# Small parts of the rwkv projections' weights: split beforehand into DRAM instead of split on arrival

## The chip, the cores and the metric

The kernel runs on one core of a Trainium2 chip. The metric is the time of one execution on the device in microseconds (us); for a kernel it is the median of its runs. PE is the matrix engine, PEld its weight loads, DVE, ACT and POOL are the vector, scalar and GpSimd engines, and SP is the queue from which nearly all DMAs are issued.

## The reference, cut to what matters

Two blocks of two layers each run one after the other on 256 tokens of 1024 features. The first block's second layer is an rwkv mixer; between its first layer's mixer and it lies a squared-relu MLP on tokens and context (512 columns in all):

```
x = x + gt_m * squared_relu_mlp(modulate(x, sh_m, sc_m), mlp_w1[layer], mlp_w2[layer])
ctx = ctx + cgt_m * squared_relu_mlp(modulate(ctx, ...), ...)
...
o_l, o_c = rwkv_mixer(h_l, h_c, rw_mu[j], rw_w_rkv[j], rw_w0[j], rw_w1[j], ...)
```

The mixer forms six mixtures of each token with its neighbours and multiplies them by weights: k, r and v (1024 x 1024 each), and the narrow w1, a1, g1 and g2.

## The kernel before, in words

Every product with weights is done in three passes of float32r: a weight tile is split into a large part `wh` (a cast) and a small part `wl` (the tile less that cast), the activations likewise into `mh` and `ml`, and `mm3` sums wh·mh, wh·ml and wl·mh (L162, L163, L164 are the three matmuls). A tile of weights is 128 x 1024 once split (`HLC` columns) and 128 x 2048 as most are loaded (`WCOL` columns, 1 MB).

In the first MLP the order is that of the code and of the tile framework. ACT casts (L71), DVE subtracts (L72), SP loads (L48). A feature tile of the hidden layer takes 8 weight units; its relu is on ACT (L1871), and ACT also casts the result to `dh` (L167). The results lie in two PSUM banks, `g`. The next layer's modulation (`ada`) is a thread: its matmuls (L1343, 16 tiles) are put between the MLP's first products, a group of four tiles at a time, and its last groups run behind the MLP.

In the rwkv projections (`rwkv_in`) a planner, `Weave`, takes up threads of requests in the order in which it reckons that engines come free, and writes the instructions in that order; each engine and queue then works strictly in it. Threads there are the norm and mixing (`ri_front` L2038 to L2049, `ri_mix` L2063 to L2069), the weights (`wv_weights`), the products (`ri_products`), and behind them the "items" (L2297 to L2425), the elementwise work on decays and keys that prepares the scan. `wv_weights` loads into two raw tiles of 2048 columns, casts on ACT (L445), and subtracts on DVE (L453), or, for each second tile of k and r, on POOL (L450). Split tiles lie in four slots called `whl`, each given back once the last product with it is placed. Some elementwise steps may go to either DVE or POOL; the planner chooses by its own clock.

k's product begins with a lead of four feature tiles, features of the mixture outer and tiles inner: it takes a unit of each of the weight tiles k0 to k3 for every mixed feature. `lww` and `lwa` are the parts of two more small weights (in_rw_w, in_rw_a), needed only behind the products w and a; they pass through the same raw tiles (loaded at L2255, cast at L2257, subtracted at L2260).

Of the kernel before, what the change touches and what calls it, by code (L numbers as in the profile page):

```python
# [13 lines left out]
ALU = mybir.AluOpType  # L14
# [15 lines left out]
class Stream:  # L30
    """A weight matrix as a row of [128, nb] units, loaded in tiles of WCOL
    columns and split into two float32r parts whose sum is exact."""
# [47 lines left out]
class KB:  # L80
    HLC = 1024

    def __init__(self, tc, ins, out, dbg=None):
# [3 lines left out]
        self.pend = []  # L87

# [24 lines left out]
    def open_psum(self, **banks):  # L113
        """all of PSUM: banks per pool"""
# [4 lines left out]
    def open_gemm(self, n=4):  # L119
        """the pools of the products with weights"""  # L120
# [21 lines left out]
    def row_in(self, name, n, pool=None):  # L142
        """a row of n numbers, the same in all partitions"""
# [8 lines left out]
    def act_set(self, after, name):  # L152
        """load a named activation table right behind an instruction"""
# [5 lines left out]
    def mm3(self, ps, wh, wl, xh, xl, start, stop):  # L159
        """ps += (wh + wl).T @ (xh + xl) in three float32r passes"""  # L160
# [9 lines left out]
    def begin(self, g):  # L170
        """runs a generator's first part; the others follow behind later products"""
# [12 lines left out]
    def gemm_a(self, st, nt, kt, xh, xl, evac, n_cols=T, lead=0, cuts=2):  # L184
        """features of the result on partitions; st units [128k, 128n], n outer;
        the first lead tiles take the products in cuts parts, a part of all of them at a time"""
# [9 lines left out]
        for n in range(lead, nt):  # L196
            ps = self.psg.tile([P, 512], F32, name="g")
            o = ps[:, :n_cols]
            for k in range(kt):
                wh, wl = st.next()  # L200
                self.mm3(o, wh, wl, xh(k), xl(k), k == 0, k == kt - 1)
            evac(n, o)

    def gemm_b(self, st, nt, kt, pairs, xh, xl, evac, between=None):
        """tokens of the result on partitions; st units [128k, 256], n outer; one
        bank holds two token tiles"""
# [14 lines left out]
    def rstd_tok(self, sums, n, width, scale, eps):  # L221
        """(sums * scale + eps) ** -0.5 on a [128, n] tile"""
# [7 lines left out]
    def sumsq(self, pool, xs, kt):  # L230
        """for each x the sum over its feature tiles of x squared: [128, T], the partitions still to add"""
# [12 lines left out]
    def rstd_from(self, acc, n_feat):  # L244
        """token-major 1/rms [128, 2] from the squares' partial sums"""
# [5 lines left out]
    def bcast_tok(self, rs, pool, col=0, n=2):  # L251
        """rs [128 tokens, n] -> [128, n * 128], the same row in all partitions"""
# [11 lines left out]
class Phase:  # L264
    """pools of one phase: tag -> number of buffers, opened together"""
# [20 lines left out]
def bc(ap, axis, n):  # L286
    """ap with a new axis of n equal entries at free position axis"""
# [6 lines left out]
class Weave:  # L294
    """Emits threads of work, each a generator of requests, in the order in which the
    engines would take them up. A request comes before the instructions it stands for:
    (engine, us and the latency behind it), ("any", us by engine), ("take", slot) and ("give", (slot, index)), ("set", event) and
    ("wait", event), ("later", us), ("spawn", generator) or ("spawn", generator, us by which it
    lets others go before)."""
# [10 lines left out]
    def settle(self, th):  # L310
        """one request of a thread that needs no engine; whether it could be met"""
# [69 lines left out]
    def load(self, end):  # L381
        """the array's work in the window before a time"""
# [4 lines left out]
    def keep(self, end, work, after=None):  # L387
        """products of no use ahead of work up to a time, where the array's clock would drop"""
# [5 lines left out]
    def add_warm(self, at, n, after=None):  # L394
        """n products of 64 columns"""
# [14 lines left out]
class Second(KB):  # L410
    WOVEN = None

# [1 line left out]
    def wv_open(self, cut=1):  # L414
        """the weights' tiles, held; those loaded into cut in parts"""
        raw = [self.raw.tile([P, WCOL], F32, name="raw") for _ in range(2)]
# [5 lines left out]
    def wv_weights(self, streams, ring="", shared=()):  # L422
        """weights in their order, loaded and split"""
# [36 lines left out]

    def wv_unit(self, name, nb, u):
        """waits for a unit of weights; its parts"""
# [7 lines left out]
    def wv_done(self, name, nb, us, last, ring=""):  # L470
        """gives back the tiles of weights whose last unit is among us"""
# [6 lines left out]
    def pre_norm(self, ph, gain, x=None, tagx="xn"):  # L478
        """splits x * gain; returns the parts and the squares' partial sums"""
# [76 lines left out]
            # gating  # L556
# [36 lines left out]
            # layer norm of g over its 512 features  # L593
# [28 lines left out]
    def gelu(self, ph, out, x, n):  # L622
        """0.5 x (1 + tanh(sqrt(2/pi) (x + 0.044715 x^3))); overwrites x's scratch"""
# [78 lines left out]
    def mem_load(self):  # L702
        """the memory and the squares' sums, for both layers"""
# [2437 lines left out]
```

## Time and profile before

| | us |
|---|---|
| median of 3 runs | 2858.17 |
| lowest and highest run | 2854.01, 2858.56 |
| span of the profiled execution | 2854.8 |
| first MLP | 421 to 783 |
| rwkv projections | 783 to 1054 |

The span goes from the first to the last instruction of one profiled execution. Around the span there is no separate figure: the median of the runs is 3.4 us above it, and a sum made on the span is carried to the median by adding these 3.4 us. A busy engine is no proof of a bound: the stages have different limits, so the sections below go stage by stage.

### The profile page before, as it was taken

What the parts mean: (1) busy time and instruction counts of PE and PEld (TensorE: products, weight loads), DVE (VectorE), ACT (ScalarE), POOL (GpSimd) and SP (SyncE); (2) the same over time, 40 slices, a digit from 0 to 9 for tenths busy, and PEclk for the clock granted to TensorE, in tenths of its full rate; (3) what the DMA queues carried; (4) which work ended last, traced back from release to release, by engine and by line L of the source; (5) the groups of instructions that cost most, each with busy time, mean ns of one, the idle gap of its engine ahead of it and who ended that gap; (6) DMA issues with size and microseconds to landing.
All of it is one profiled execution on the core that took longest, in us unless ns stands there. A gap on an engine that the chain in (4) does not pass through costs nothing.

```text
span 2854.8 us, 52905 instructions
## 1 busy us (share of the span) xinstructions
PE 2654.0 (93%) x22052; PEld 2362.1 (83%) x22052; DVE 1763.1 (62%) x2885; ACT 1297.4 (45%) x2358; POOL 402.5 (14%) x392
## 2 busy tenths in 40 slices
PE   5999999999968879887899999999999999799999
PEld 3977567888757666765899999998999999798999
DVE  4453564334386966885774665776665665765764
ACT  3344333223245541675553544555444444655443
POOL 1210100000044552342100001011001001311100
PEclk9999989999978889998999999999999999999999
DMA  7244735223223675323455455433455554233554
GB/s 274 89 156 152 260 126 191 103 89 104 83 72 107 226 228 114 81 68 96 139 186 179 170 183 198 163 134 119 167 188 177 178 186 172 96 105 110 177 178 148
DMA packets 108142, 426.29 MB, mean 149 GB/s; under 512 B 14334, under 2 KB 50430, under 8 KB 66046
## 3 DMA queue, kind: packets, MB, share of 16 engines
q1 hardware_dynamic: 107326, 420.76, 43.1%
q8 instruction: 173, 2.83, 0.4%
q10 hardware_dynamic: 576, 2.15, 0.2%
q14 instruction: 67, 0.55, 0.1%
HBM read 397.68 MB, written 24.13 MB: 148 GB/s over the span
## 4 chain that ended last, share of the span: by engine, by line
PE 78%; DVE 13%; ACT 4%; POOL 2%; issue 2%; DMA 1%; SPq 0%; ACTq 0%; DVEq 0%; POOLq 0%
PE g L162 20%; PE g L163 20%; PE g L164 20%; PE pG L162 2%; PE pG L163 2%; PE pG L164 2%; DVE pr L2605 2%; DVE N L2607 2%; PE d L1343 2%; PE pX L2623 1%; DVE wl L72 1%; PE pA L2551 1%; POOL acc L495 1%; DVE we L2558 1%; POOL rs L227 1%
## 5 line engine op out<-in xcount | busy, mean ns | idle before, releaser
L72 DVE TENSOR_TENSOR wl<-raw,wh 128x1024 fp32r<-128x1024 f32 x512 | 626.9, 1225 | 427.7 <-ACT wh L71 425.5
L71 ACT CAST wh<-raw 128x1024 fp32r<-128x1024 f32 x512 | 535.2, 1047 | 638.0 <-PE g L163 546.2
L163 PE MATMUL g<-xnl,wh 128*128 128x256 f32 x1504 | 427.9, 285 | 1.0 <-DVE xnl L168 1.0
L162 PE MATMUL g<-xnh,wh 128*128 128x256 f32 x1504 | 427.4, 285 | 1.3 <-ACT xnh L167 1.3
L164 PE MATMUL g<-xnh,wl 128*128 128x256 f32 x1504 | 427.9, 285 | 0.0
L162 PE MATMUL g<-hh,wh 128*128 128x256 f32 (+1 forms) x1216 | 374.4, 308 | 4.9 <-ACT wh L71 3.4
L164 PE MATMUL g<-hh,wl 128*128 128x256 f32 (+1 forms) x1216 | 373.3, 307 | 0.7 <-DVE wl L72 0.7
L163 PE MATMUL g<-hl,wh 128*128 128x256 f32 (+1 forms) x1216 | 373.9, 308 | 0.0
L162 PEld LDWEIGHTS g<-xnh,wh 128*128 128x128 f32 x1504 | 290.5, 193 | 1.7 <-ACT xnh L167 1.7
L163 PEld LDWEIGHTS g<-xnl,wh 128*128 128x128 f32 x1504 | 290.6, 193 | 1.5 <-DVE xnl L168 1.5
L164 PEld LDWEIGHTS g<-xnh,wl 128*128 128x128 f32 x1504 | 290.7, 193 | 0.0
L162 PEld LDWEIGHTS g<-hh,wh 128*128 128x128 f32 x1216 | 234.6, 193 | 17.5 <-ACT wh L71 4.0
L163 PEld LDWEIGHTS g<-hl,wh 128*128 128x128 f32 x1216 | 234.3, 193 | 14.2 <-DVE hl L1382 2.5
L164 PEld LDWEIGHTS g<-hh,wl 128*128 128x128 f32 x1216 | 234.1, 193 | 12.5 <-issue 1.7
L495 POOL TENSOR_TENSOR acc<-acc,sq 128x256 f32<-128x256 f32 x63 | 65.8, 1045 | 863.5 <-ACT sq L494 381.2
L162 PE MATMUL g<-dh,wh 128*128 128x512 f32 (+1 forms) x512 | 172.0, 336 | 0.0
L163 PE MATMUL g<-dl,wh 128*128 128x512 f32 (+1 forms) x512 | 172.0, 336 | 0.0
L164 PE MATMUL g<-dh,wl 128*128 128x512 f32 (+1 forms) x512 | 172.0, 336 | 0.0
L2623 PE MATMUL pX<-ident 128*128 128x256 f32 (+3 forms) x388 | 106.9, 386 | 32.8 <-DVE N L2607 17.9
L163 PE MATMUL g<-wl,hh 128*128 128x256 f32 x448 | 128.4, 287 | 6.9 <-DVE wl L72 6.9
L162 PE MATMUL g<-wh,hh 128*128 128x256 f32 x448 | 131.2, 293 | 3.3 <-ACT wh L71 3.2
L164 PE MATMUL g<-wh,hl 128*128 128x256 f32 x448 | 127.8, 285 | 0.0
(590 smaller groups left out, 5961.7 us busy)
## 6 DMA issues: line engine op xcount, KB each, us to landing
raw<-in_w_mlp SPq DMA_DIRECT2D x64, 1024.0 KB, 4.8
raw<-in_w_ada SPq DMA_DIRECT2D x48, 1024.0 KB, 6.3
raw<-in_w_pre_gu SPq DMA_DIRECT2D x44, 1024.0 KB, 4.8
raw<-in_w_post_gu SPq DMA_DIRECT2D x44, 1024.0 KB, 4.8
raw<-in_w_pre_down SPq DMA_DIRECT2D x22, 1024.0 KB, 4.8
raw<-in_w_post_down SPq DMA_DIRECT2D x22, 1024.0 KB, 4.8
raw<-in_w_ab SPq DMA_DIRECT2D x14, 1024.0 KB, 4.9
d_bk<-h SPq DMA_DIRECT2D x16, 512.0 KB, 3.0
```

The costliest lines, as they stand in the source:

```text
L71: nc.scalar.copy(h[:, :w], r)
L72: nc.vector.tensor_tensor(l[:, :w], r, h[:, :w].bitcast(F32), op=ALU.subtract)
L162: mm(ps, wh, xh, start=start, stop=False)
L163: mm(ps, wh, xl, start=False, stop=False)
L164: mm(ps, wl, xh, start=False, stop=stop)
L227: nc.gpsimd.tensor_tensor(rs[:, :n], ms[:, :n], self.mhalf[:, :n], op=ALU.pow)
L495: nc.gpsimd.tensor_tensor(acc, acc, sq, op=ALU.add)
L1343: nc.tensor.matmul(ps[32 * j : 32 * j + 32], self.cpad[:, k0 + j, 30 - 2 * n : 62 - 2 * n], raw[:, j * 512 : (j + 1) * 512], start=n == 0 ...
L2551: nc.tensor.matmul(ps[64:, i], bk[:64, i0 + i], we[0][:64, :W, i0 + i], start=True, stop=True)
L2605: nc.vector.tensor_tensor(pr, bc(N[:, k + 1 :, k], 2, k), bc(N[:, k, :k], 1, m), op=ALU.mult)
L2607: row = nc.vector.tensor_tensor(N[:, k + 1 :, :k], N[:, k + 1 :, :k], pr, op=ALU.add)
L2623: mm = self.nc.tensor.matmul(o, self.ident, bc(self.ident[:, :64], 1, cols // 64), start=True, stop=True)
```

## The change

Thirty tiles of 128 x 1024, all of k, w1, a1, g1, g2, r and v, get their small parts during the first MLP. A new generator `lows` loads a tile (a DMA of ACT's queue), casts it on ACT, subtracts on DVE and stores the small part to DRAM (again ACT's queue). It moves by one step per eight products of the MLP. In the projections, `wv_ready` loads the raw tile from SP as before, casts it on ACT, and reads the small part from DRAM by a DMA of POOL's queue. No subtraction of these weights is left there. Raw tiles there become two of 1024 columns (one tile cut in two), and the space of the second one becomes a fifth `whl` slot. So that the space for `lows` is free, the rest of the modulation thread is drained at the beginning of the MLP. The planner's order changes with all this.

```diff
 class KB:
+        self.side = None
 def gemm_a(...):
                 self.mm3(o, wh, wl, xh(k), xl(k), k == 0, k == kt - 1)
+                if self.side and k % 8 == 7:
+                    next(self.side, None)
...
+    def wv_ready(self, streams):
...
+                raw = yield "take", "raw"
+                nc.sync.dma_start(w, self.i[src][t, :, c : c + n])
+                q = yield "take", "whl"
+                h, l = self.wt["whl"][q]
+                yield "Pool", 0.5, 0.0
+                nc.gpsimd.dma_start(l[:, :n], self.low[src][t, :, c : c + n])
...
+                    yield "ACT", 0.12 + 0.83 * n / 1024
+                    nc.scalar.copy(h[:, :n], w)
+                    yield "give", ("raw", raw)
...
 def mlp(...):
             self.modulate(ph, self.xs[:ns], mods, 3, self.split_shift(hh, hl), between, (4, 2, 4))
+            if behind:
+                behind()
...
+class Lows(First):
+    LOWS = [("w_rw_k", 64 * P), ("w_rw_w1", 8 * P), ("w_rw_a1", 8 * P), ("w_rw_g1", 16 * P), ("w_rw_g2", 8 * 256), ("w_rw_r", 64 * P),
+            ("w_rw_v", 32 * 256)]
+    def lows(self, ph):
...
+        tile = lambda: ph.tile("lw", [P, self.HLC], F32R)
+        def weights(src, at):
...
+            a = tile()
+            w = a.bitcast(F32)
+            nc.scalar.dma_start(w, self.i[src][t, :, c])
+            yield
+            h = ph.tile("lh", [P, self.HLC], F32R)
+            nc.scalar.copy(h, w)
+            nc.vector.tensor_tensor(a, w, h.bitcast(F32), op=ALU.subtract)
+            yield
+            nc.scalar.dma_start(self.low[src][t, :, c].bitcast(F32), a.bitcast(F32))
+        parts = [weights(n, at) for n, w in self.LOWS for at in range(0, w, self.HLC)]
+        for j in range(len(parts) + 3):
+            for g in parts[max(j - 3, 0) : j + 1]:
+                next(g, None)
+            yield
...
 def rwkv_in(...):
-            self.wv_open(2)
-            w = self.weave = Weave(raw=2, whl=4, ...)
+            self.wv_open(2, 1)
+            more = self.raw.tile([P, WCOL], F32R, name="raw")
+            self.wt["whl"].append([more[:, : self.HLC], more[:, self.HLC :]])
+            w = self.weave = Weave(raw=2, whl=5, G=4, L=2, f=2, xg=3, o=3, kk=3, it=4)
...
-            w.add(self.wv_weights(self.STREAMS, shared="kr"), 0.5)
+            w.add(self.wv_ready(self.STREAMS), 0.5)
...
 def run(self):
+                def behind():
+                    for _ in self.ada:
+                        pass
+                    pa.__exit__(None, None, None)
+                    self.side = self.lows(es.enter_context(self.phase("lo", side=RIGHT, lw=4, lh=2)))
+                self.mlp(0, a0[1], 2, self.ada, behind)
+                for _ in self.side:
+                    pass
```

Line numbers move with it: the MLP's relu L1871 is L1909 in the changed kernel, its cast L167 is L168, the mixing's L2067 is L2141, the items' L2362 is L2436, the power L2220 is L2294. New are L477 (raw load), L482 (DMA of the small part), L488 (cast), and in the MLP L1943 (load), L1946 (cast), L1949 (store).

**ACT's order in the first MLP.** Before, the steady round (r is a relu's result, dh its cast, wh a cast of the MLP's weights):

```order
L1871 ACTIVATE r<-g 128x512 [waits PE_49]
L167 CAST dh<-r 128x512 [waits DVE_49]
L71 CAST wh<-raw 128x1024 [waits DMAHW2_49]
L71 CAST wh<-raw 128x1024 [waits PE_49,Activation_49]
L1871 ACTIVATE r<-g 128x512 [waits PE_49,Activation_49]
L167 CAST dh<-r 128x512 [waits DVE_49]
```

Of the change, in the same place, from the first of the loads of `lows` on (adrow is the last copy of the modulation; lw and lh are the tiles of `lows`):

```order
L1943 DMA lw<-in_w_rw_k 128x1024 [waits DMAHW5_49,DMAHW4_49,DMAHW6_49,DMAHW2_49,DMAHW0_49]
L1943 DMA lw<-in_w_rw_k 128x1024 [waits DMAHW5_49,DMAHW3_49,DMAHW7_49,DMAHW1_49,PE_49]
L1943 DMA lw<-in_w_rw_k 128x1024
L1946 CAST lh<-lw 128x1024 [waits DMAHW6_49,Activation_49]
L1946 CAST lh<-lw 128x1024 [waits DMAHW7_49]
L1943 DMA lw<-in_w_rw_k 128x1024
L1949 DMA low_w_rw_k<-lw 128x1024 [waits DVE_49] x2
L1946 CAST lh<-lw 128x1024 [waits DMAHW0_49,Activation_49]
L1909 ACTIVATE r<-g 128x512 [waits PE_49]
L1946 CAST lh<-lw 128x1024 [waits DMAHW1_49,Activation_49]
```

The relu in the middle now stands behind three casts of `lows`, each of which waits for a load, and behind two stores, each of which waits for DVE. Later in the MLP the order has come to a steady round:

```order
L1943 DMA lw<-in_w_rw_w 128x1024 [waits DMAHW0_49]
L71 CAST wh<-raw 128x1024
L1949 DMA low_w_rw_k<-lw 128x1024 [waits DVE_49]
L1909 ACTIVATE r<-g 128x512 [waits PE_49]
L1946 CAST lh<-lw 128x1024 [waits DMAHW6_49,Activation_49]
L168 CAST dh<-r 128x512 [waits DVE_49]
```

Each round has one load, one store and one cast of `lows` in ACT's queue between the MLP's own three instructions, and the cast waits for the load that opens the round.

**SP's order at the start of the projections.** Before (raw tiles of k hold two tiles of 1024 each):

```order
L434 DMA raw<-in_w_rw_k 128x2048 [waits DVE_49,DMAHW1_49,Activation_49,Pool_49]
L1999 DMA sel<-in_c_sel 128x256 [waits PE_49]
L434 DMA raw<-in_w_rw_k 128x2048 [waits DVE_49,DMAHW2_49,Activation_49,Pool_49]
L2255 DMA raw<-in_rw_w 128x1024 [waits DMAHW7_49,DVE_49]
L2255 DMA raw<-in_rw_a 128x1024 [waits DMAHW3_49,DMAHW1_49,DVE_49]
```

Of the change, from k2's raw load on:

```order
L477 DMA raw<-in_w_rw_k 128x1024 [waits DMAHW7_49,Activation_49]
L2073 DMA sel<-in_c_sel 128x256 [waits DVE_49,PE_49]
L2329 DMA raw<-in_rw_w 128x1024 [waits DMAHW0_49,Activation_49]
L2329 DMA raw<-in_rw_a 128x1024 [waits DMAHW6_49,DMAHW3_49,Activation_49]
L477 DMA raw<-in_w_rw_k 128x1024 [waits DMAHW5_49,DVE_49]
L477 DMA raw<-in_w_rw_k 128x1024 [waits DMAHW6_49,DVE_49]
L477 DMA raw<-in_w_rw_k 128x1024 [waits DMAHW7_49,DMAHW1_49,Activation_49]
```

The loads of in_rw_w and in_rw_a stood behind all of k; now they take the two raw slots behind k2, and the loads of k3 and k4 wait for DVE to have done with them.

**ACT's order there.** Of the change, from the cast of k2 on (mh is a mixed feature's cast; there are 16 of the first mixture in all, and the last two stand here; `raw` as a target is the fifth slot):

```order
L488 CAST wh<-raw 128x1024 [waits DMAHW3_49]
L2141 CAST mh_6462<-f_6678 128x512 [waits DVE_49]
L2331 CAST lww<-raw 128x1024 [waits DMAHW5_49,Activation_49]
L2141 CAST mh_6462<-f_6677 128x512 [waits DVE_49]
L2141 CAST mh_6462<-f_6678 128x512 [waits DVE_49]
L2331 CAST lwa<-raw 128x1024 [waits DMAHW6_49,Activation_49]
L2141 CAST mh_6462<-f_6677 128x512 [waits DVE_49]
L2141 CAST mh_6462<-f_6678 128x512 [waits DVE_49]
L488 CAST wh<-raw 128x1024 [waits DMAHW7_49]
L488 CAST raw<-raw 128x1024 [waits DMAHW0_49]
```

The cast of k3 now comes behind the 16th mh. Before, the cast of k3 stood behind the fourth mh (here the third cast and the fourth):

```order
L445 CAST wh<-raw 128x1024 [waits DMAHW2_49]
L2043 ACTIVATE h<-xg_6388,mods_103 128x256 [waits Pool_49]
L2043 ACTIVATE h<-xg_6389,mods_103 128x256 [waits Pool_49]
L2067 CAST mh_6265<-f_6390 128x512 [waits DVE_49]
L2067 CAST mh_6265<-f_6391 128x512 [waits DVE_49]
L2043 ACTIVATE h<-xg_6388,mods_103 128x256 [waits DVE_49]
L445 CAST wh<-raw 128x1024
L2043 ACTIVATE h<-xg_6387,mods_103 128x256 [waits Pool_49]
```

**POOL's order ahead of the items.** Before, behind the last instruction on the mixture of g (L2220 is the power for the keys' norm, L2362 the first step of the items):

```order
L2069 TENSOR_TENSOR ml_6268<-f_6494,mh_6267 128x256 [waits PE_49,Activation_49,Pool_49]
L2220 TENSOR_TENSOR o_6497<-o_6497,mhalf 128x16 [waits DVE_49]
L2220 TENSOR_TENSOR o_6497<-o_6497,mhalf 128x16 x3
L450 TENSOR_TENSOR wl<-raw,wh 128x1024 [waits DMAHW0_49,PE_49,Activation_49]
L450 TENSOR_TENSOR wl<-raw,wh 128x1024 [waits DMAHW1_49,Activation_49]
L2069 TENSOR_TENSOR ml_6268<-f_6494,mh_6267 128x512 [waits Activation_49]
L450 TENSOR_TENSOR wl<-raw,wh 128x1024 [waits DMAHW2_49,PE_49,Activation_49]
L450 TENSOR_TENSOR wl<-raw,wh 128x1024 [waits DMAHW3_49,PE_49,Activation_49]
L2362 TENSOR_SCALAR xx<-xx 128x512 [waits Activation_49] x2
```

Of the change:

```order
L2143 TENSOR_TENSOR ml_6463<-f_6677,mh_6462 128x256 [waits Activation_49]
L482 DMA raw<-low_w_rw_r 128x1024 [waits DMASW1_49,PE_49]
L2322 TENSOR_TENSOR llw<-o_6681,lhw_6689 64x512 [waits Activation_49,Pool_49]
L2294 TENSOR_TENSOR o_6680<-o_6680,mhalf 128x16 [waits DMAHW2_49,DVE_49]
L2294 TENSOR_TENSOR o_6680<-o_6680,mhalf 128x16 x2
L482 DMA wl<-low_w_rw_r 128x1024 [waits DMASW2_49,PE_49]
L2294 TENSOR_TENSOR o_6680<-o_6680,mhalf 128x16
L482 DMA wl<-low_w_rw_r 128x1024 [waits DMASW3_49,PE_49]
L482 DMA wl<-low_w_rw_r 128x1024 [waits DMASW4_49,PE_49]
L482 DMA wl<-low_w_rw_r 128x1024 [waits DMASW5_49,PE_49]
L482 DMA raw<-low_w_rw_r 128x1024 [waits DMASW6_49,PE_49]
```

Each of the DMAs waits for PE to be done with the slot's last tile, and POOL's later instructions wait behind it; here one stands ahead of the last power.

## Rows read from the trace of the kernel before

**Rows 1.** The page: busy time, share and instructions of each engine.

```profile
PE 2654.0 (93%) x22052; PEld 2362.1 (83%) x22052; DVE 1763.1 (62%) x2885; ACT 1297.4 (45%) x2358; POOL 402.5 (14%) x392
```

**Rows 2.** Busy time (instructions) of each engine by stretch, clock, DMA share, GB/s.

```profile
421.00:521.00 100.00, 99.95 (x448) 74.36 (x449) 49.28 (x74) 38.62 (x59) 0.00 (x0) 0.97 0.46 169
521.00:600.00 79.00, 79.00 (x350) 65.40 (x350) 25.72 (x31) 16.93 (x17) 0.00 (x0) 1.00 0.27 94
...
866.00:940.00 74.00, 61.86 (x338) 49.62 (x337) 56.59 (x77) 44.04 (x77) 35.48 (x17) 0.83 0.31 108
940.00:1054.00 114.00, 101.64 (x586) 80.04 (x585) 101.28 (x121) 61.87 (x96) 67.41 (x72) 0.90 0.69 233
```

**Rows 3.** The same view for L453's instructions alone.

```profile
783.00:836.00 53.00, 4.03 (x2) 0.71 0.19 68
...
940.00:1054.00 114.00, 12.65 (x8) 0.90 0.69 233
sum 271.00, DVE 33.23; mean DVE 8.31
```

**Rows 4.** Timeline of PE around the start of k's product.

```profile
816.18 0.80 PE L164 MATMUL pG<-mh,wl 128*128 128x512 f32 x1 [15.32 <-POOL wl L450]
816.77 0.63 PE L162 MATMUL pG<-mh,wh 128*128 128x512 f32 x1
...
820.42 0.39 PE L162 MATMUL pG<-mh,wh 128*128 128x512 f32 x1
```

**Rows 5.** Timeline of DVE in the mixing: start, duration, idle before.

```profile
812.41 4.27 DVE L2049 SCALAR_TENSOR_TENSOR xx<-xx,h 128x512 f32<-128x512 f32 x2
816.60 3.52 DVE L2063 SCALAR_TENSOR_TENSOR f<-xx,rwv,h 128x512 f32<-128x512 f32 x2
820.04 0.68 DVE L2049 SCALAR_TENSOR_TENSOR xx<-xx,h 128x512 f32<-128x512 f32 x1
...
833.38 1.41 DVE L2063 SCALAR_TENSOR_TENSOR f<-xx,rwv,h 128x512 f32<-128x512 f32 x2
```

**Rows 6.** The chain of waits from 860 to 942: start, us, what.

```profile
874.24 1.14 DVE wl L453
...
917.52 2.40 POOL wl L450
919.92 2.51 issue
...
925.32 3.54 DVE f L2063 x2
```

**Rows 7.** DMA issues: queue, count, KB each, median us to landing.

```profile
raw<-in_w_mlp SPq DMA_DIRECT2D x64, 1024.0 KB, 4.8
...
raw<-in_w_mla_uq SPq DMA_DIRECT2D x6, 512.0 KB, 3.4
```

**Rows 8.** Timeline of ACT in the first MLP.

```profile
456.74 0.59 ACT L1871 ACTIVATE r<-g 128x512 f32<-128x512 f32 x1
458.73 0.62 ACT L167 CAST dh<-r 128x512 fp32r<-128x512 f32 x1 [1.40 <-DVE r L1872]
461.17 1.05 ACT L71 CAST wh<-raw 128x1024 fp32r<-128x1024 f32 x1 [1.82 <-PE g L163]
...
466.61 1.05 ACT L71 CAST wh<-raw 128x1024 fp32r<-128x1024 f32 x1 [1.87 <-PE g L163]
```

**Rows 9.** Timeline of ACT's queue at the start of the program.

```profile
1.64 0.45 ACTq L1410 DMA_DIRECT2D xT<-in_xT  x1
```

**Rows 10.** Timeline of PE behind the first MLP.

```profile
782.25 1.92 PE L1343 MATMUL d<-raw,cpad 128*32 128x512 f32 x16
784.88 1.08 PE L1351 MATMUL t<-sel,adrow 128*128 128x32 f32 x8 [0.71 <-ACT adrow L1347]
785.79 1.12 PE L248 MATMUL t<-ones,acc 128*128 128x1 f32 x8
```

**Rows 11.** Groups of instructions from 783 to 1054: POOL.

```profile
L450 POOL TENSOR_TENSOR wl<-raw,wh 128x1024 fp32r<-128x1024 f32 x8 | 20.7, 2596 | 43.6 <-ACT wh L445 43.6
```

More of the change, by code (lines that the diff above doesn't have):

```diff
@@ L411, with wv_open @@
     WOVEN = None
-    def wv_open(self, cut=1):
-        raw = [self.raw.tile([P, WCOL], F32, name="raw") for _ in range(2)]
+    def wv_open(self, cut=1, raws=2):
+        raw = [self.raw.tile([P, WCOL], F32, name="raw") for _ in range(raws)]
         self.wcut = n = WCOL // cut
@@ L456, in parts @@
                     yield "give", ("raw" + ring, raw)
+                yield "spawn", parts()
+                j += 1
+    def wv_ready(self, streams):
+        nc = self.nc
+        hl = self.HLC
+        self.weave.events["parts", 0] = 0.0
+        j = 0
+        for name, src, units, nb in streams:
+            for at in range(0, units * nb, hl):
+                n = min(hl, units * nb - at)
+                raw = yield "take", "raw"
+                w = self.wt["raw"][raw][:, :n]
+                t, c = divmod(at, WCOL)
+                yield "DMA", n / 1024 * 1.3, 0.0
+                nc.sync.dma_start(w, self.i[src][t, :, c : c + n])
+                q = yield "take", "whl"
+                h, l = self.wt["whl"][q]
+                yield "Pool", 0.5, 0.0
+                yield "DMA", n / 1024 * 1.3, 0.0
+                nc.gpsimd.dma_start(l[:, :n], self.low[src][t, :, c : c + n])
+                def parts(name=name, at=at, n=n, h=h, q=q, j=j, w=w, raw=raw):
+                    yield "later", 2.0
+                    yield "wait", ("parts", j)
+                    yield "ACT", 0.12 + 0.83 * n / 1024
+                    nc.scalar.copy(h[:, :n], w)
+                    yield "give", ("raw", raw)
+                    yield "set", ("parts", j + 1)
+                    self.have[name, at // hl] = q
+                    yield "set", ("weights", name, at // hl)
                 yield "spawn", parts()
@@ L1853, in mlstm, with mlp @@
         self.drain()
-    def mlp(self, l, mods, ns, between=None):
+    def mlp(self, l, mods, ns, between=None, behind=None):
         nc = self.nc
@@ L1884, in mlp @@
                             lambda k: dh[:, k], lambda k: dl[:, k], ev2, w)
-class Third(First):
+class Lows(First):
+    LOWS = [("w_rw_k", 64 * P), ("w_rw_w1", 8 * P), ("w_rw_a1", 8 * P), ("w_rw_g1", 16 * P), ("w_rw_g2", 8 * 256), ("w_rw_r", 64 * P),
+            ("w_rw_v", 32 * 256)]
+    def lows(self, ph):
+        nc = self.nc
+        dt = lambda name, shape: self.dram.tile(shape, F32R, name=name)
+        self.low = {n: dt("low_" + n, [-(-w // WCOL), P, WCOL]) for n, w in self.LOWS}
+        tile = lambda: ph.tile("lw", [P, self.HLC], F32R)
+        def weights(src, at):
+            t, c = divmod(at, WCOL)
+            c = slice(c, c + self.HLC)
+            a = tile()
[12 more added lines that the diff above has]
+            yield
+class Third(Lows):
     C = 32
@@ L1957, in rwkv_in @@
             nc.vector.tensor_tensor(self.hmk, bc(self.hm, 1, KT), bc(self.rv[:, 12], 2, 2), op=ALU.mult)
-            self.wv_open()
-            w = self.weave = Weave(raw=2, whl=4, G=4, L=2, f=2, xg=3, o=3, kk=3, it=4)
+            self.wv_open(2, 1)
+            more = self.raw.tile([P, WCOL], F32R, name="raw")
+            self.wt["whl"].append([more[:, : self.HLC], more[:, self.HLC :]])
+            w = self.weave = Weave(raw=2, whl=5, G=4, L=2, f=2, xg=3, o=3, kk=3, it=4)
             w.slots.update(o2=[], bk=[], r=[])
@@ L2937, in run @@
             a1 = self.adaln_open(1)
-            with self.phase("ad", side=RIGHT, c=1, araw=2, adp=1) as pa:
-                self.cond_load(pa)
-                self.araw, self.adp = pa.pools["araw"], pa.pools["adp"]
-                self.ab_mixer(a0, a1)
-                self.mlp(0, a0[1], 2, self.ada)
-                for _ in self.ada:
+            pa = self.phase("ad", side=RIGHT, c=1, araw=2, adp=1).__enter__()
+            self.cond_load(pa)
+            self.araw, self.adp = pa.pools["araw"], pa.pools["adp"]
+            self.ab_mixer(a0, a1)
+            with ExitStack() as es:
+                def behind():
[5 more added lines that the diff above has]
+                for _ in self.side:
                     pass
+                self.side = None
             self.rwkv(a1[1])
```

## The prediction

> **What bounds the kernel now.** I read the busy times first, then the same by stretches, and in each stretch what ended the waits. PE is busy 93% of the span and DVE 62% [rows 1], but the two stages that the change touches have different limits. In the first MLP, PE never stops: 99.95 of 100 us, then 79.00 of 79 [rows 2], with ACT busy 21% and DVE 33% from 521 to 600 and the DMA engines at 0.27. Whatever is added there off PE costs nothing, as long as ACT and DVE hand PE its tiles in time; any lateness is paid in full. In the projections PE is not the limit: 61.86 of 74 us from 866 to 940, at a mean clock of 0.83, and from 940 to 1054 DVE is busy 101.28 of 114 [rows 2]. So a DVE subtraction taken away there can be worth its length, and one on POOL what its result is waited for. Three places show it. The product of k stands still for 15.32 us until 816.18, for a small part that POOL made [rows 4]. The chain from 860 to 942 goes through a POOL subtraction, then DVE steps of the mixture [rows 6]. And while POOL subtracts, DVE's own steps are longer: two L2063 take 3.52 us at 816.60 and 1.41 at 833.38; two L2049 take 4.27 us where one takes 0.68 later [rows 5].
>
> **What is removed, and what of it lay on the path.** 22 subtractions, 33.23 us, leave DVE [rows 3], 8, 20.7 us, leave POOL [rows 11]. They are not one saving; I go by stretch.
>
> *The items, 940 to 1054.* DVE sets the pace, and loses 12.65 us [rows 3]. In the new order the planner moves a net six elementwise steps of this stretch from POOL to DVE, at the 0.7 us of one step of half a tile [rows 5] some 4 us. That leaves −8.5. The same tiles are now read twice over (whole and small part): sixteen tiles of r and v, 0.5 MB each, are 8 MB more on DMA engines that are already 0.69 busy at 233 GB/s [rows 2]. At that rate 8 MB would be 34 us of transfer; it fits in the 31% left only nearly, so I add 2.5 us of late tiles. Together −6, bounds −13 (nothing moved costs anything) and +5.
>
> *The chain from 866 to 940.* On it stand the POOL subtraction (2.40) and the 2.51 us behind it, and three of DVE's L453 at 1.14 each [rows 6], so 8.3 us; DVE steps lengthened beside POOL: two L2063 at 3.54 against 1.41 [rows 5, 6], 2.1 us, and by my estimate some 5 us at three others of the same kind. The rest, some 1.6, are mixture steps that the planner now gives to DVE rather than to slow POOL. Sum −17; bounds −5 (only the subtractions on DVE, with the small parts landing as late as POOL made them) and −20.
>
> **What is moved.** *The start of k's product.* Here the change works against itself. The raw tiles are half as large, so the loads of in_rw_w and in_rw_a take the two slots behind k2, and k3's load waits for DVE's subtraction of the first. ACT has k3's cast behind all 16 mh. PE takes a unit of k0, k1, k2 and k3 for each mixed feature, so it cannot pass its fourth unit before that cast. Before, PE went on from 816.18. DVE's last two L2063 of this mixture start at 833.38 and take 1.41 [rows 5]: the 16th feature is there at 834.8. From this I take off 4.03 us of subtractions [rows 3] and the stretching at 812 and 816, (4.27 − 1.36) + (3.52 − 1.41) = 5.0 us, add 2.4 for the two subtractions of lww and lwa that now come into the mixing, and 0.6 + 1.0 for the last mh and the cast: 829.8 to 831.4. PE starts 15 us later than 816.18. All features are mixed by then, so PE runs through, but it ran without a stop from 820 before too, and gives nothing back: +15. Bounds: +10 when POOL's work vanishes from DVE entirely, +18 when none of the 5.0 comes back.
>
> *The modulation.* Two groups of it and the transposes, 1.92 + 1.08 us of PE [rows 10], come from behind the MLP into its start. There PE is full, so +2.7; behind it the chain from 782.25 to the norm's matmul at 785.79 [rows 10] becomes shorter by 1.2, since squares and sums remain.
>
> **What is added.** *In the MLP*, 30 tiles with a load, a cast, a store on ACT and a subtraction on DVE. By busy time this is free: a round of the MLP is 5.44 us (461.17 to 466.61), of which ACT uses 1.05 + 0.59 + 0.62 [rows 8]; a cast more and two issues at 0.45 [rows 9] make 4.2. But ACT works in order, and its cast waits for a load that ACT issued in the same round. A round on ACT then lasts the load's latency L plus cast 1.05 and dh 0.62 and an issue 0.45, which is L + 2.1. A 512 KB load has a median of 3.4 [rows 7], so 5.5, just the round of PE. 1 MB takes 4.8, so each 512 KB that is in the way costs 1.4 [rows 7]. In the steady state there is little in the way; for a mean L of 3.5 the delay is 0.15 a round, 1.5 us for ten rounds. At the start three loads go out together, the third lands 3.4 + 2 × 1.4 = 6.2 us after its issue, and the relu behind its cast comes some 6.6 us late by my reckoning; the second bank of PSUM covers most of a round, which leaves 2.7 us of PE idle. Two rounds later a cast of the MLP's own weights stands behind the cast of the fifth load: another 3.1 (an estimate by the same steps). After a stop the matmuls run slower, 0.63 us at 816.77 against 0.39 at 820.42 [rows 4]: up to 2 us for both. So the MLP with the modulation: 2.7 − 1.2 + 2.7 + 3.1 + 2 + 1.5 = +11. Bounds: +2, when ACT's lateness stays within the banks; +24, when L is 4.5, 1.1 us a round over 12 rounds more.
>
> *On POOL*, 30 DMAs. No row has a DMA issued there. Below stands SP's and ACT's issue, 0.45 [rows 9], above the subtraction that it replaces, 2.6 [rows 11]; I take 1 us, since nothing is computed, and then POOL, busy 67.41 of 114 us in the items [rows 2], hides it.
>
> The Trainium skill speaks against this queue: "SBUF — State Buffer", section "SBUF: two separate sides" (the box on the "DVE blocks DMA" trap), says that GpSimd itself writes the descriptors of such a DMA and cannot while DVE holds the shared port, and the section "A bandwidth-pool intuition that's wrong" gives about 3.1 us instead of 0.62. By it the sixteen DMAs of r and v alone would hold POOL for an estimated 50 us, and the sum would end near rival D. No row here shows such a DMA; the long DVE steps of [rows 5] only show that the two engines get in each other's way.
>
> **Sum.** +11 (MLP) + 15 (k's start) − 17 (866 to 940) − 6 (items) = +3 us on the span of 2854.8; from its median, 3.4 above, 2858.2 + 3 = 2861.
>
> **Rivals.**
> *A, the sum as it stands:* 2861, within 0.2% (5.7 us, about what a measurement can tell from no change). 0.30.
> *B, the MLP hides its guest:* ACT's casts are late but the banks hold, +2 instead of +11, and k's start is +10. Then 2858.2 + 2 + 10 − 17 − 8 = 2845; with the items at their best 2838. For it: ACT's 21%. Against it: an in-order engine waiting on a load in each round. 0.33.
> *C, ACT's round is longer than PE's.* Place: the MLP's first half, 13 rounds. Price: L over 3.4 is paid round by round; it decides from L = 3.8 on, where 0.4 × 12 = 5 us are added. With L = 4.5 the MLP costs 24, so 2874. For it: each round now has 0.5 MB of weights, 0.5 MB loaded and 0.5 MB stored, some 290 GB/s against 94 before [rows 2]. 0.20.
> *D, POOL's queue:* a DMA that waits for a slot, or for its descriptors, holds the power and the items behind it. At 2.6 rather than 1 us for each of ten DMAs before and among the first items, +16: 2877. For it: the order has one ahead of the last power and eight ahead of the items. Against it: POOL's idle time. 0.17.
>
> Faster is B, 0.33; slower C and D, 0.37. The range leaves out the ends of B and D: 2836 to 2885.
>
> **What would show it.** MLP: PE idle behind the fourth relu, ACT's rounds between 5.4 and 6 us, the stage 9 to 13 us longer. Projections: PE waits for a large part (ACT), not POOL's small part, and starts k's product about 15 us after the corresponding moment; no DVE step over 2 us beside a POOL subtraction; 866 to 940 in some 57 us, the items in about 108. Wrong would be: no idle of PE in the MLP (then B), a mean round above 5.9 (C), waits of PE or DVE for POOL's DMAs (D).

## The result, and the profile after

The change makes the kernel slower: a median of 2881.38 us (2876.22 to 2882.96, 4 runs) against 2856.09 us of the kernel before on the same chip (4 runs), a ratio of 1.0084 with a 95% interval of 1.0069 to 1.0100. The profiled execution has a span of 2880.7 us, 25.9 more than before. The time lies inside the stated range (2836 to 2885) but 20 us above the number, near the rivals that forecast slower (2874 and 2877) and not at the sum.

The page of the changed kernel, busy time of each engine; PE's row is to be read beside [rows 1]:

```profile
PE 2661.4 (92%) x22052; PEld 2364.0 (82%) x22052; DVE 1760.8 (61%) x2901; ACT 1323.6 (46%) x2388; POOL 381.7 (13%) x406
```

DVE's busy time hardly falls, since the thirty subtractions came back in the MLP. Where the 25.9 us lie shows best between four instructions that both kernels have: the first normalised feature in the MLP (ACT, `hh`), the first matmul of the norm behind it (PE, `t<-ones,acc`), the first step of the items (DVE, L2362, now L2436), and the first copy of `cf` on DVE at their end. Of the changed kernel, their rows of the timelines of ACT, PE and DVE:

```profile
422.31 1.56 ACT L1417 ACTIVATE hh<-xg,mods 128x256 fp32r<-128x256 f32 x3
```

```profile
801.22 1.05 PE L251 MATMUL t<-ones,acc 128*128 128x1 f32 x8 [1.54 <-DVE acc L244]
```

```profile
957.18 0.43 DVE L2436 TENSOR_SCALAR xx<-xx 128x512 f32<-128x512 f32 x1 [2.21 <-ACT xx L2433]
...
1079.14 0.19 DVE L2371 COPY cf<-pM 128x32 f32<-128x32 f32 x1 [0.70 <-PE pM L2474]
```

Before, they start at 419.83, 785.79 [rows 10], 935.98 and 1053.15. The differences, for both kernels and for the experiments below, each from its one profiled execution (us):

| kernel | MLP | norm to items | items | both latter |
|---|---|---|---|---|
| before | 366.0 | 150.2 | 117.2 | 267.4 |
| changed | 378.9 | 156.0 | 122.0 | 277.9 |
| e1_mlp_only | 381.6 | 151.4 | 123.2 | 274.6 |
| e2_projections_only | 365.2 | 157.6 | 121.7 | 279.3 |
| e3_cast_free | 386.3 | 145.8 | 133.5 | 279.3 |
| e4_sp_queue | 380.1 | 127.2 | 134.3 | 261.5 |
| e5_ahead | 373.9 | 159.0 | 121.6 | 280.5 |
| e6_v_eighth | 381.5 | 157.7 | 117.2 | 274.8 |
| e7_drain_only | 367.4 | 151.7 | 117.2 | 269.0 |
| e8_sp_ahead | 376.2 | 127.6 | 134.4 | 262.0 |
| e9_later | 369.0 | 127.0 | 132.1 | 259.1 |

So 13 us are lost in the MLP, 6 on the way to the items, 5 in the items; the remaining 2.5 of the 25.9 lie ahead of the MLP, where the code is the same (that start lies between 416.0 and 422.3 in all these executions), and are a difference between executions. One execution thus carries a few us of chance; stages are compared here, and medians used for the verdicts.

**The MLP.** PE's waits from 452 to 482 (line waited for, us in total, times, longest):

```profile
PE g L163 <- ACT r L1909: 4.1, 1, 4.1
PE g L163 <- ACT wh L71: 1.6, 1, 1.6
```

ACT's timeline shows what the relu (L1909) stood behind:

```profile
459.34 2.56 ACTq L1943 DMA_DIRECT2D lw<-in_w_rw_k  x3
465.02 1.05 ACT L1946 CAST lh<-lw 128x1024 fp32r<-128x1024 f32 x1 [5.25 <-DMA lw<-in_w_rw_k]
466.77 1.05 ACT L1946 CAST lh<-lw 128x1024 fp32r<-128x1024 f32 x1 [0.70 <-DMA lw<-in_w_rw_k]
...
467.36 2.08 ACTq L1949 DMA_DIRECT2D low_w_rw_k<-lw  x2
469.54 1.04 ACT L1946 CAST lh<-lw 128x1024 fp32r<-128x1024 f32 x1 [1.72 <-DVE lw L1947]
470.49 0.59 ACT L1909 ACTIVATE r<-g 128x512 f32<-128x512 f32 x1
...
478.27 1.05 ACT L1946 CAST lh<-lw 128x1024 fp32r<-128x1024 f32 x1 [2.81 <-DMA lw<-in_w_rw_k]
```

Three loads go out at 459.34; the first cast waits 5.25 us for its load, the third 1.72 us for DVE, and only behind it, at 470.49, comes the relu, for whose PSUM bank PE waits 4.1 us. Before, ACT had a relu and two casts in a round here, and 3 us idle [rows 8]. The stretches show how far it goes (columns as in [rows 2]):

```profile
452.00:482.00 30.00, 24.32 (x103) 17.00 (x99) 11.45 (x14) 11.47 (x16) 0.00 (x0) 0.89 0.80 294
482.00:521.00 39.00, 38.48 (x169) 31.45 (x168) 25.06 (x28) 20.52 (x27) 0.00 (x0) 1.00 0.77 274
521.00:600.00 79.00, 78.55 (x343) 63.99 (x343) 44.03 (x49) 34.00 (x38) 0.00 (x0) 1.00 0.82 288
```

PE stands still for 5.7 us of 30 from 452 to 482, but for 0.5 of 39 and 0.5 of 79 behind it: there its tiles come nearly in time although the DMA engines are 0.82 busy at 288 GB/s where it was 0.27 at 94 [rows 2]. Most of the rest of the loss is in the matmuls themselves. The whole stage of the kernel before, then that of the change, then two of its stretches behind the stop (PE's busy time is the third number of a row, the clock the third from the end):

```profile
419.83:785.79 365.96, 364.04 (x1624) 291.72 (x1625) 146.33 (x201) 111.95 (x158) 0.18 (x2) 0.99 0.33 116
```

```profile
422.31:801.22 378.91, 369.49 (x1625) 292.82 (x1625) 180.10 (x237) 140.15 (x188) 0.18 (x2) 0.98 0.54 191
...
470.00:475.00 5.00, 3.87 (x9) 3.10 (x10) 4.20 (x5) 3.39 (x6) 0.00 (x0) 0.55 0.90 347
475.00:480.00 5.00, 4.76 (x16) 3.43 (x15) 1.34 (x2) 1.72 (x3) 0.00 (x0) 0.76 0.68 230
```

Of the 13 us, 7.5 are idle time of PE (9.4 against 1.9), and 5.4 are longer matmuls, as many as before. Right behind the wait for the relu the granted clock is 0.55, mostly the lower of its two levels (1.2 and 2.4 GHz), then 0.76; it is 1.00 again from 482 on. By these two rows the clock accounts for some 2.9 us (an estimate: 3.87 × 0.45 + 4.76 × 0.24). In e7 and e9 below, where PE never waits longer than 1.7 us in the stage, it is busy 364.6 us, nearly as before.

**The start of k's product.** POOL's, ACT's and PE's timelines around it:

```profile
824.65 1.17 POOL L2112 TENSOR_TENSOR xg<-ctx,rb 128x256 f32<-128x256 f32 x1
825.76 0.77 POOL L482 DMA_DIRECT2D wl<-low_w_rw_k  x1
826.56 1.30 POOL L2121 TENSOR_TENSOR xx<-h 128x512 f32<-128x512 f32 x1
827.82 1.10 POOL L482 DMA_DIRECT2D wl<-low_w_rw_k  x2
```

```profile
831.02 1.04 ACT L488 CAST wh<-raw 128x1024 fp32r<-128x1024 f32 x1
...
835.53 1.04 ACT L488 CAST wh<-raw 128x1024 fp32r<-128x1024 f32 x1
...
837.69 1.04 ACT L488 CAST wh<-raw 128x1024 fp32r<-128x1024 f32 x1
...
848.63 1.04 ACT L488 CAST wh<-raw 128x1024 fp32r<-128x1024 f32 x1
```

```profile
832.11 0.79 PE L163 MATMUL pG<-mh,wh 128*128 128x512 f32 x1 [27.43 <-ACT wh L488]
...
849.73 0.80 PE L163 MATMUL pG<-mh,wh 128*128 128x512 f32 x1 [9.29 <-ACT wh L488]
```

The last row is the step foreseen: PE waits 9.29 us for k3's cast, which comes behind all mixed features, and goes on at 849.73. From the norm's matmul that is 48.5 us (801.22 to 849.73) where it was 30.4 (785.79 to 816.18 [rows 4, 10]): 18 us later. But k0's cast, at 831.02, is late already, though its raw tile was loaded in the MLP: in ACT's order it stands behind seven casts of mixed features. Just ahead of it POOL issues its first DMAs, at 825.76 and 827.82, behind its steps of the mixing. That was not in the prediction, and experiments 3 and 4 take it up.

**The items.** Before, of the change, and of e1 below, which has the order of before in this stage:

```profile
936.00:1053.20 117.20, 104.78 (x589) 80.79 (x587) 104.91 (x124) 64.38 (x99) 69.00 (x73) 0.89 0.69 235
```

```profile
957.20:1079.10 121.90, 112.74 (x577) 84.29 (x578) 96.77 (x119) 65.36 (x102) 61.85 (x75) 0.83 0.79 261
```

```profile
953.30:1076.50 123.20, 110.41 (x590) 84.54 (x587) 104.17 (x123) 64.84 (x100) 68.73 (x73) 0.85 0.66 223
```

DVE is 96.77 us busy, 8 less than before; yet the items did not become shorter. PE stands idle less, 9.2 us against 12.4, but nearly the same matmuls (577 and 589) take 112.74 us instead of 104.78, at a granted clock of 0.83 instead of 0.89. The clock moves between executions too, 0.85 in e1. In the three profiles with the order of before it is 0.85 to 0.89, in the four with the change's order 0.81 to 0.84. DVE's waits in this stretch:

```profile
DVE xx L2463 <- ACT xx L2461: 8.3, 5, 4.2
DVE kk L2397 <- PE pL L2395: 5.7, 5, 2.4
```

The two largest, 8.3 and 5.7 us, are for a scaling step of ACT (L2461) and for PE's small matmuls that spread a factor of the keys (L2395).

**POOL's DMAs.** The line that issues them (duration in ns, least, median, most; then when):

```profile
L482 POOL DMA_DIRECT2D wl<-low_w_rw_k x7: 527/535/769, 825.8 to 871.3; - x7
...
L482 POOL DMA_DIRECT2D wl<-low_w_rw_v x6: 527/592/615, 950.1 to 1033.1; - x6
...
DMA to landing us min/median/max: 4.0/5.7/9.4
```

An issue takes 0.53 to 0.77 us, and a part lands 4.0 to 9.4 us after it, 5.7 in the median.

### The profile page after: what moved, and what is told of

Read it like the earlier page. It is cut to its first block, busy times and chain, and to the rows that moved or that the text cites. A ratio compares the mean times of both kernels' runs of the same rounds, so it can differ in the third digit from the quotient of the medians.

```text
span 2880.7 us, 53124 instructions
## 1 busy us (share of the span) xinstructions
PE 2661.4 (92%) x22052; PEld 2364.0 (82%) x22052; DVE 1760.8 (61%) x2901; ACT 1323.6 (46%) x2388; POOL 381.7 (13%) x406
## 4 chain that ended last, share of the span: by engine, by line
PE 76%; DVE 13%; ACT 4%; DMA 3%; POOL 2%; issue 2%; SPq 0%; ACTq 0%; POOLq 0%; DVEq 0%
PE g L163 19%; PE g L165 19%; PE g L164 19%; PE pG L163 2%; PE pG L164 2%; PE pG L165 2%; DVE pr L2679 2%; DVE N L2681 2%; PE d L1379 2%; PE pX L2697 1%; DVE wl L72 1%; PE pA L2625 1%; POOL acc L531 1%; DVE we L2632 1%; DMA d_r<-o 1%
## 5 line engine op out<-in xcount | busy, mean ns | idle before, releaser
L230 POOL TENSOR_TENSOR rs<-ms,mhalf 128x2 f32<-128x2 f32 (+2 forms) x53 | 54.5, 1030 | 609.8 <-DVE ms L228 609.8
```

Source lines behind the costliest of these rows:

```text
L230: nc.gpsimd.tensor_tensor(rs[:, :n], ms[:, :n], self.mhalf[:, :n], op=ALU.pow)
```

## The experiments

Times are medians beside the kernel before on the same chip in the same batch: 2861.37 us for the first four, 2859.41 for the next four, 2862.28 for the last.

**1 and 2: the two halves of the change, each alone.**

```diff
 e1: rwkv_in
-            w.add(self.wv_ready(self.STREAMS), 0.5)
+            w.add(self.wv_weights(self.STREAMS, shared="kr"), 0.5)
 e2: run() as before; in wv_ready
-                nc.gpsimd.dma_start(l[:, :n], self.low[src][t, :, c : c + n])
+                nc.gpsimd.dma_start(l[:, :n], self.i[src][t, :, c : c + n].bitcast(F32R))
```

> The small parts are made in the first MLP and stored, but the projections split their weights themselves as before, so the stored parts are not read. Theory (the terms are separate, and the MLP's own is what the changed trace shows, 15.4 us from the start of the MLP to the first step of the mixing): 2856 + 15 = 2871. Rival (half of what the MLP loses is given back because later stages wait for something else): 2863 or less.

> The first MLP and the modulation as before; the projections read a second tile of 512 KB from DRAM by POOL's queue instead of subtracting, but that tile is the weight itself (the small part's values are left out). Theory (separate terms, by the changed trace: +18 at the start of k's product, -12 from there to the items, +5 in the items): 2856 + 11 = 2867. Rival (the stored parts land late because their stores in the MLP and the loads collide): the projections gain here, 2850 or less.

Measured: 2882.05 us for the MLP alone, ratio 1.0070 (1.0050 to 1.0089); 2867.70 for the projections alone, ratio 1.0016 (1.0000 to 1.0032). The MLP's half costs 20 us by itself, most of the 25 that the change loses and 5 more than the theory's 15; its profile has 15.6 of them in the MLP and 6 in the items, whose code is that of before, and whether the MLP's half lengthens these, one profile cannot tell. The projections' half costs 4 to 6, less than the 11 expected, and is not clear of no change at its lower end; 2867.70 meets the number 2867 only because before takes 5 us more in this batch. Both rivals fall: nothing of the MLP's loss is given back later, and the projections do not gain when the MLP is left alone. Their start of k's product is as late as in the change (830.12, 49.0 us behind the norm's matmul at 781.16).

**3 and 4: what makes k's product late.** Thread and queue of the small part's load:

```diff
 e3: wv_ready
-                q = yield "take", "whl"
-                yield "Pool", 0.5, 0.0
-                nc.gpsimd.dma_start(l[:, :n], self.low[src][t, :, c : c + n])
+                def lowpart(l, ...):
+                    yield "wait", ("pq", j)
+                    yield "Pool", 0.5, 0.0
+                    nc.gpsimd.dma_start(l[:, :n], self.low[src][t, :, c : c + n])
+                    yield "set", ("low", j)
                 def parts(...):
+                    q = yield "take", "whl"
+                    yield "spawn", lowpart(l)
                     nc.scalar.copy(h[:, :n], w)
                     yield "give", ("raw", raw)
+                    yield "wait", ("low", j)
 e4: as e3, but in lowpart
-                    yield "Pool", 0.5, 0.0
-                    nc.gpsimd.dma_start(l[:, :n], self.low[src][t, :, c : c + n])
+                    nc.sync.dma_start(l[:, :n].bitcast(F32), self.low[src][t, :, c : c + n].bitcast(F32))
```

> The whole change, but in the planner's thread for the weights a tile's cast and the next raw load no longer come behind the tile's DMA on POOL's queue; that DMA is a thread of its own. The loads of in_rw_w and in_rw_a thereby fall behind k4 and the casts of k0 to k3 among the first mixed features. Theory (k's start waits for k3's cast, which the plan put late because POOL's turn came first): k's product starts 14 to 17 us earlier, still held by POOL's DMAs, which come behind its steps of the mixing; 2881 - 15 = 2866. Rival (two half-sized raw tiles are too few, whatever the order): 2878 to 2884.

> As the one before, but the small parts are loaded by SP's queue instead of POOL's. Theory (POOL's place in the plan is what makes the small parts late): k's product starts with the mixing, 25 to 30 us earlier than in the change, and POOL's 16 us of DMA issues are gone: 2852. Rival (SP works in order, and the loads that wait for free slots hold back the small transfers of the items): 2866 or more, with the items longer than 122 us.

Measured: 2879.70 us, ratio 1.0058 (1.0037 to 1.0079), for the first; 2869.46, ratio 1.0026 (1.0016 to 1.0037), for the second. In the first, the casts of k0 to k4 do stand among the first mixed features, and what PE waits for is now the small part. POOL's timeline, then PE's, of that run:

```profile
827.33 4.18 POOL L2131 TENSOR_TENSOR xx<-h 128x512 f32<-128x512 f32 x3 [0.82 <-ACT h L2127]
831.45 2.37 POOL L484 DMA_DIRECT2D wl<-low_w_rw_k  x4
```

```profile
837.46 0.79 PE L165 MATMUL pG<-mh,wl 128*128 128x512 f32 x1 [16.91 <-DMA wl<-low_w_rw_k]
```

POOL's DMAs come behind its last step of the mixing, PE has the first part 6 us later, and k's product goes on 31.5 us behind the norm's matmul (805.92 to 837.46), 17 earlier than in the change: the size that was expected for k's start. The two raw tiles are not too few. With SP's queue the longest such wait is 7.30 us, for the first mixed feature, and k2 and k3 come in 18 and 21 us behind the norm's matmul (800.17 to 818.23 and 820.83). PE's timeline of that run:

```profile
818.23 0.79 PE L163 MATMUL pG<-mh,wh 128*128 128x512 f32 x1 [1.42 <-ACT wh L496]
...
820.83 0.79 PE L163 MATMUL pG<-mh,wh 128*128 128x512 f32 x1 [0.96 <-ACT wh L496]
```

But the first gives its 17 us back: norm to items falls from 156.0 to 145.8, and the items grow from 122.0 to 133.5. So does the second, in part: 127.2 and 134.3. The sum of both stages is 279.3, 261.5 and, in the change, 277.9. An earlier start of the items is not an earlier end; of the 28 us that the second gains at k3's unit 16 are left at the items' end. So both theories are right about k's start and miss the time, 2866 by 14 us and 2852 by 17. Each measured time lies where the rival had it, but not for the rival's reason: in the first the raw tiles are not what is waited for, and its items are as long as the second's, 133.5 us, without a small part on SP's queue.

**5 and 7: what the MLP loses.** A cast one step later after its load, and the modulation's drain alone:

```diff
 e5: lows
             nc.scalar.dma_start(w, self.i[src][t, :, c])
             yield
+            yield
-                    self.side = self.lows(... lw=4, lh=2)
+                    self.side = self.lows(... lw=5, lh=1)
 e7: run(), with rwkv_in as in e1
                     pa.__exit__(None, None, None)
-                    self.side = self.lows(...)
```

> The whole change, but in the MLP a tile is cast one step later after its load (one tile more for the loads, one less for the casts). Theory (ACT, in order, waits for a load issued in the same round, at the start in front of the relu): the waits of PE for the relu and for the MLP's large parts, 5.7 us in the change, fall to 2 or less, and the MLP is 4 to 8 us shorter: 2881 - 6 = 2875. Rival (the MLP's loss is the traffic of 0.5 MB in and 0.5 MB out per round, which delays the MLP's own weights): no change, 2878 to 2884.

> Only the modulation is drained at the start of the first MLP; no small parts are made, and the projections split their weights as before. Theory (the modulation moves 2.7 us of PE into the MLP and takes 1.2 off the tail; the rest of the MLP's loss is the small parts): 2861 + 2 = 2863 on a chip where before takes 2861. Rival (the drain takes PE's start out of step and costs most of the 15 us by itself): 2870 or more.

Measured: 2878.10 us, ratio 1.0066 (1.0044 to 1.0088); 2860.16, ratio 1.0003 (0.9985 to 1.0021). The drain alone costs 1.4 us of the stage (367.4), the 1.5 that the prediction had for it, and nothing that the medians show; its rival falls. The later cast makes the MLP shorter, 373.9 us (376.2 in e8, which has the same MLP) against 378.9 to 386.3 in the five executions that have the MLP's code as in the change; PE's waits for relu and large part become 2.0 and 1.6 us, in sum 3.6 and not the 2 or less expected. The median falls by 3 us, the ratio by 5, but the intervals overlap, and 2878.10 lies at the rival's edge: that the kernel as a whole gains is not shown by this run alone.

**6: the traffic in the items.**

```diff
+                m = n // 8 if name == "v" else n
-                nc.gpsimd.dma_start(l[:, :n], self.low[src][t, :, c : c + n])
+                nc.gpsimd.dma_start(l[:, :m], self.low[src][t, :, c : c + m])
```

> The whole change with the same order of all instructions, but the eight loads of v's small parts move an eighth of the bytes (the rest of these small parts is left out). Theory (the items grew from 117 to 122 us because 261 GB/s leave the small transfers late): the items shrink by 4 to 8 us, 2875. Rival (the items are set by PE, busy 114 of 123 us at a clock of 0.83, and by the order): within 2 us, 2879 to 2883.

Measured: 2882.56 us, ratio 1.0085 (1.0058 to 1.0113), the change's own, and within the rival's 2879 to 2883. In the profiled execution the items take 117.2 us instead of 122.0, but the median does not move, and 5 us are what one execution of the items differs from another: e1, with the order of the kernel before in this stage, took 123.2 where before took 117.2. The traffic is not shown to cost anything; the interval is some 8 us wide to either side and does not exclude the 4 of the theory.

**8 and 9: both together, and a later beginning.** The SP version with the cast one step later, then with eight empty steps ahead of the first tile:

```diff
 e9: lows, on top of e4 and e5
+        for j in range(8):
+            yield
         for j in range(len(parts) + 4):
```

> The small parts loaded by SP's queue, casts not behind them in the plan, and in the MLP the cast one step later after its load: the two changes of the earlier runs together. Theory (the MLP's loss and the late start of k's product are separate): the gain on the SP version of 2869 is that of the cast one step later alone, 4 to 8 us: 2863, no faster than before. Rival (a shorter MLP and shorter projections add up to more than either): 2855 or less.

> As the two changes together, but the small parts begin eight steps later, behind the modulation's traffic. Theory (what is left of the MLP's loss, 10 us there, is the start, where modulation, MLP weights and the first tiles meet on ACT's queue and on the DMA engines): the MLP loses 3 to 6 us instead of 10, and the kernel comes to 2856 where before takes 2859, 0.1% faster or the same. Rival (the loss is spread over the MLP, by the traffic): the MLP still loses 9 or more, 2862.

Measured: 2862.04 us, ratio 1.0013 (0.9999 to 1.0027), as the theory had it, so its rival falls; and 2854.32 us (12 runs) against 2862.28, ratio 0.9974 (0.9959 to 0.9989): 0.26% faster than the kernel before, and faster than the change. Its MLP takes 369.0 us, 3.1 more than before, and PE's longest waits there are 1.5 us for the first normalised features, as before, 1.7 for the modulation's own weights and 1.5 for the norm's sums at the end. Two of its stretches (columns as in [rows 2]):

```profile
450.00:480.00 30.00, 28.31 (x136) 21.58 (x135) 15.20 (x18) 13.54 (x19) 0.00 (x0) 1.00 0.79 282
...
520.00:600.00 80.00, 80.00 (x355) 66.27 (x354) 43.27 (x46) 33.52 (x35) 0.00 (x0) 1.00 0.84 292
```

PE is busy 80.00 of 80 us while the DMA engines are 0.84 busy at 292 GB/s. The rival, that the traffic spreads the loss over the MLP, falls.

The items stay long in all four runs whose k product starts early (e3, e4, e8, e9: 132.1 to 134.4 us). DVE has two long waits there that it does not have in the change. Of e8:

```profile
DVE lww L2344 <- ACT lww L2341: 9.9, 1, 9.9
DVE xx L2480 <- DMA f<-d_r: 9.8, 1, 9.8
```

The one is for a cast of in_rw_w, the other for r's product on its way through DRAM; both are 8.7 to 10.4 us in each of the four, and in the change DVE waits 1.1 us in all for the second. Whether they are what lengthens the items, no run separates.

## Why the prediction was right or wrong

**The sign and the range.** By stages the sum had +11 in the MLP, 15 − 17 = −2 up to the items and −6 in them; the profile shows +13, +6 and +5. That the kernel could become slower had a chance of 0.37, and the range reached to 2885, so the time lies in it; but the number stood for "no change", and neither C nor D, which forecast such a time, happened as described. That the range holds is in part luck. Two of its figures also do not follow from its terms: k3's cast comes to 829.8, 13.6 us behind 816.18, and no term stands for the rest up to 831.4; and B's 2838 is 2840 by the items' best of −13.

**The MLP, +11 (bounds +2 and +24).** Right in its mechanism: ACT's order, a relu behind three casts and two stores at the start, a large part of the MLP's weights two rounds later. The waits were foreseen as 2.7 and 3.1 us and are 4.1 and 1.6, the same in sum. Too small was the term for slower matmuls behind a stop: up to 2 us were taken, and PE is busy 5.4 us longer, of which the drain has 0.6 (364.62 in e7). The stage lost 13 in the change's own execution and 14 to 20 in four others of the same code; e1 gives 20 for the kernel as a whole. Experiments 5 and 9 take the loss apart: a cast later after its load saves some 7 us in the mean (e5 and e8 against the five), a later beginning another 5 to 7. The last moves the median too (ratio 1.0013 to 0.9974), but what it avoids at the start, the modulation's traffic or the order of ACT's queue, no run separates. Experiment 7 bears out the modulation's own 1.5.

**Rival C, rounds longer than PE's,** is not what happened, though the latency L of the loads of `lows` was well above the 3.8 from which it was to decide (least, median, most; 3.4 in [rows 7]):

```profile
DMA to landing us min/median/max: 3.1/5.4/8.0
```

What failed is the sum L + 2.1 for a round of ACT. Its rows later in the MLP:

```profile
548.15 1.05 ACT L1946 CAST lh<-lw 128x1024 fp32r<-128x1024 f32 x1 [3.02 <-DMA lw<-in_w_rw_r]
548.17 0.34 ACTq L1943 DMA_DIRECT2D lw<-in_w_rw_r  x1
549.10 1.05 ACT L71 CAST wh<-raw 128x1024 fp32r<-128x1024 f32 x1
...
553.99 1.05 ACT L1946 CAST lh<-lw 128x1024 fp32r<-128x1024 f32 x1 [3.84 <-DMA lw<-in_w_rw_r]
554.01 0.34 ACTq L1943 DMA_DIRECT2D lw<-in_w_rw_r  x1
```

The next load is issued as the cast begins, not behind it, and the MLP's own cast runs while it is under way. A round of ACT is then about L alone, 5.8 us here and 5.4 at the median, beside PE's 5.44; PE lost 1 us behind 482.

**k's start, +15.** The size was nearly right (18) and so was what PE waits for. The cause was only half of it. The prediction named the raw tiles taken by in_rw_w and in_rw_a; experiment 3 shows that these stood there because the thread of the weights had to wait for POOL's turn in the plan, tile by tile, and that the small part would have come late in any case.

**866 to 940, −17.** Norm to items grew by 5.8 with 18 lost at k's start, so 12 were won back, five fewer than the term; which of its parts came, no run separates.

**The items, −6.** This step failed. They became no shorter (121.6 to 122.0 us in three executions of the change's order and 117.2 in e6, 117.2 to 123.2 in three of the order before), and the experiments that start them 28 to 29 us earlier end them no more than 16 to 19 earlier (261.5 and 259.1 against 277.9 for both stages). DVE did lose the 8 us of work, net, that the term foresaw; it waited instead, 25 us in all where it had waited 12. It was read as the bound because it was busy 101 of 114 us [rows 2]. But PE was busy as long, 101.64 in the same row, and had only 12.4 us of idle time to give; it gave 3 of them, and its matmuls took 8 longer at the lower clock. With two engines both near nine tenths, work taken from one moves the wait to the other. Why the clock is lower is open: PE had less idle time than before, not more, and no run here isolates it. The 2.5 us taken for traffic are not shown by experiment 6.

**POOL's DMAs.** The 1 us taken for an issue was 0.53 to 0.77. The Trainium skill ("SBUF — State Buffer", section "A bandwidth-pool intuition that's wrong") has such a DMA take about 3.1 us beside a DVE copy, which the prediction took as time that POOL is held. None of the 30 issues held POOL for so long; whether DVE's steps here are of the kind that the page speaks of, no run shows. Rival D was right that POOL's queue matters, by another way: not a DMA that holds the items, but DMAs that come late behind POOL's own work, in the plan and on the engine.

## What to carry to other kernels

Work that is moved onto idle engines is free by its busy time only if it does not wait in an in-order engine in front of something that the bound engine needs: put a load and its use a step further apart, and try a later beginning where another thread still has its traffic. In a planned order, a transfer on a busy engine's queue delays not only itself but every later request of its thread; here a thread of its own moved the wait without a gain that the medians show, and SP's queue besides took 12 us off the change's median. And where two engines are both busy nine tenths of a stretch, taking work from one of them gives its length only if the other can follow.

## What was not expected of the hardware

In e9 the first MLP kept PE at 80.00 of 80 us with the DMA engines 0.84 busy at 292 GB/s, three times the traffic of before, so the MLP's own 1 MB loads were never late there. A stop of PE of 4.1 us in the MLP was followed by granted clocks of 0.55 and 0.76 over the next 10 us, so a wait cost more than its length. A DMA issued by POOL took 0.53 to 0.77 us of POOL, and its 512 KB landed in 5.7 us in the median (the DMA engines at 261 GB/s in the items) against 5.4 for the loads of `lows` on ACT's queue (274 to 294 GB/s). And the same instructions in the same order took 117.2 and 123.2 us in the items of two executions, at clocks of 0.89 and 0.85: one profile of this stage cannot show a difference of 5 us.
